# Third attention group in sixteen residues: VectorE's 32x32 transposes in place of TensorE's, values through DRAM

## The chip, the core and the metric

The kernel runs on one core of a Trainium2 chip. Its engines are named as in the profile: PE is TensorE (PEld its weight loads), DVE is VectorE, ACT is ScalarE, POOL is GpSimd, and SP is the engine whose queue issues nearly all DMAs. The metric is the device time of one execution in microseconds. Before the change the median of three runs is 1027.51 us (1027.5 to 1027.77).

## What is computed

One layer of a decoder trunk on 512 tokens of width 1024, all in float32: a normalization, one wide projection, three token mixers side by side (dilated attention, causal pooling, a state-space scan), gates, an output projection, a convolutional feed-forward layer and a last normalization. The change touches the attention alone. It has three groups of six heads of width 64; a group has a window and a dilation.

```python
ATTN_GROUPS = ((128, 1), (512, 4), (2048, 16))
...
    """Causal attention of each query t to keys t, t-d, ..., t-steps*d.
    Positions with the same residue mod d form a subsequence on which the pattern
    is a plain causal band of width `steps`; ..."""
...
    bias = bias_table[bucket].transpose(2, 0, 1).astype(jnp.float32)
    scale = 1.0 / math.sqrt(dh)
    scores = jnp.einsum("bhnqd,bhnkd->bhnqk", qb, kb).astype(jnp.float32) * scale + bias[:, None]
    scores = jnp.where(valid[None, None], scores, -jnp.inf)
    m = jnp.max(scores, axis=-1, keepdims=True)
    p = jnp.exp(scores - m)
    l = jnp.sum(p, axis=-1)
    o = jnp.einsum("bhnqk,bhnkd->bhnqd", p, vb.astype(jnp.float32)) / l[..., None]
    lse = m[..., 0] + jnp.log(l)
```

In the third group the dilation is 16, so each of 16 residues has 32 of the 512 tokens, and a query sees only keys of its own residue.

## The kernel before

**Projections and weights.** A product in float32 is made of three passes over parts of the operands: high by high, high by low and low by high (`mm3`, line 238, from which most rows of PE come). The weights go through a pipeline of jobs: SP fetches a block (`fetch`, line 184, tile `raw`), ACT writes its high part (`cast`, line 197, tile `wh`), DVE subtracts that from it (`lows`, line 217, tile `wl`), and PE multiplies. While job n runs, the weights of job n+1 are split, those of n+2 cast and those of n+3 fetched. Two buffers hold fetched blocks, so a fetch waits for the subtraction that frees one. SP issues its DMAs in order: what stands ahead of a fetch delays it.

**What runs beside them.** Smaller work is written as generators and advanced by `step()`, which is called after each chunk of a job (8 k-blocks of the three passes, 24 matmuls). A generator yields a phase, `ROWS`, `WHOLE` or `REST`, and these phases set the order of the matmuls of the generators of one step on PE. The order of instructions on PE, ACT, DVE and POOL is the order in which the program is written; that of SP is left to the planner.

**The third group (g = 2) before.** The tokens are put in four residues mod 4 of 128 tokens each: `perm`, `grouped` and `blocked` write and read queries, keys and outputs with a step of 4 elements. The scores of a head are four 128x128 blocks, one for each residue mod 4, and the bias holds a very negative number wherever query and key differ mod 16, which is in three of four places. For each head `item` in `attend` does this, in rising steps: the scores on PE (line 768, tile `ps`, for two heads at once), the bias added on DVE (line 783, tile `sb`), the negated maximum on DVE (line 787), the exponential with its sum on ACT (line 790); then, two steps later, the four 128x128 blocks are transposed on PE (line 797, tile `pt`) and copied back from PSUM (line 798, on DVE for even heads and on ACT for odd ones). After the second head of a pair PE multiplies with the values (line 811, tile `po`), and DVE copies the result out (line 816, tile `o`). The transposes and the outputs use the same four PSUM banks as the state-space scan that runs at the same time (`SM`; rows `py`, `pyo`, `pxs`, `pst`).

**Values and bias.** The values of groups two and three come out of PE with tokens as rows; `emit` in `v_pair` (line 646) moves each block of 128 rows by four DMAs from SBUF to SBUF, so that a tile `vr` holds one residue mod 4. The bias rows (`bias_rows`) are made on PE from a constant of 896 columns and the bias table (line 554), written to DRAM as `rdram` and spread by DMAs over the partitions (line 567), 128x2x128 for each pair of heads of group three.

Of the kernel before, what the change touches and what calls it, by code (L numbers as in the profile page):

```python
# [16 lines left out]
P = 128  # L17
# [20 lines left out]
C_GATE = C_DT + SH  # L38

R_OFF = (0, 384, 640)  # L40
R_LEN = (384, 256, 256)
R_ALL = 896
STEPS = (1, 1, 4)


def _bucket(dist):
# [7 lines left out]
def _constants():  # L54
    eye = np.eye(P, dtype=np.float32)
    tri = np.triu(np.ones((P, P), np.float32))
    hot = np.zeros((BUCKETS + 1, R_ALL), np.float32)
    for (window, dil), off, n, zero, step in zip(GROUPS, R_OFF, R_LEN, (255, 127, 127), STEPS):
        for j in range(n):
            rel = (zero - j) // step  # L60
            if (zero - j) % step == 0 and 0 <= rel <= window // dil:
                hot[_bucket(rel * dil), off + j] = 1.0
            else:
                hot[BUCKETS, off + j] = NEG
    ramp = np.ones((4, 16), np.float32)
    for g in range(4):
        w = 2 << g
        for t in range(w):
            ramp[g, t] = w / (t + 1.0)
    return {"c_eye": eye, "c_tri": tri, "c_hot": hot, "c_ramp": ramp}  # L70
# [13 lines left out]
def trunk(ctx: ExitStack, tc, out, x, rel_bias, ln1_g, w_in, b_gate, w_a, pool_w, pool_scale, w_b,  # L84
# [29 lines left out]
    def SM(name):  # L114
        return psum.tile([P, S], F32, name=name, tag="sm")
# [49 lines left out]
    def after(n, it):  # L165
        for _ in range(n):
            yield
        yield from it
# [176 lines left out]
    def sevens(quarter, c, side, W, emit):  # L345

        r1, r2, r3, r5 = {}, {}, {}, {}

        def job(j, load, form, use):
            def body(ws):
                wh, wl = ws
                parts = side(j)
                for i in range(2):
                    ps = MM("pb")
                    o = slice(i * P, (i + 1) * P)
                    mm3(ps[:, :c], lambda k: wh[:, k, :], lambda k: wl[:, k, :],
                        lambda k: parts[k][0][:, o], lambda k: parts[k][1][:, o], range(4), flip=True)
                    use(i, ps[:, :c])  # L360
                step()
            new = Job([load] if load is not None else [], 4, c, body)
            new.form = form
            if load is None:
                new.load = lambda: None
            return new

        def keep(r, name):
            def use(i, ps):
                r[i] = T(name)[:, :c]  # L370
                act.copy(r[i], ps)
            return use

        def p5(i, ps):
            keep(r5, "r5")(i, ps)
            dve.tensor_tensor(r2[i], r2[i], ps, OP.add)

        def p6(i, ps):
            dve.tensor_tensor(r1[i], r1[i], ps, OP.add)
            emit(0, 1, i, r1[i], r2[i])  # L380

        def p7(i, ps):
            r3[i] = T("r3")[:, :c]
# [12 lines left out]
        yield job(1, None, lambda: one.raw, p5)  # L396
        yield job(2, None, lambda: W[1], p6)
        yield job(3, None, lambda: W[0], p7)
        yield job("A22", None, lambda: diff(two.raw, two.raw, W[1]),
                  lambda i, ps: emit(1, 0, i, r3[i], ps))  # L400
# [128 lines left out]
    def bias_rows():  # L529


        relb, hot = T("relb"), [T(f"hot{i}") for i in range(2)]

        hr, two = [T(f"hotr{i}", F32R) for i in range(2)], T("relp", F32R)
        rh, rl = two[:, :18], two[:, 18:36]
        dve.memset(relb[:, :18], 1.0)
        sp.dma_start(relb[:BUCKETS, :18], rel_bias)
        sp.dma_start(hot[0][:BUCKETS + 1, :S], c_hot[:, :S])
        sp.dma_start(hot[1][:BUCKETS + 1, :R_ALL - S], c_hot[:, S:])

        def part(tiles, lo, n):
            i = lo // S
            return tiles[i][:, lo - i * S:lo - i * S + n]

        def rows():
            rv = [T(f"rv{i}") for i in range(2)]
            rd = dram.tile([HEADS, R_ALL], F32, name="rdram")
            ps_r = [SM("psr0"), SM("psr1")]
            for g, (off, n) in enumerate(zip(R_OFF, R_LEN)):
                lo = off  # L550
                while lo < off + n:
                    m = min(off + n, (lo // S + 1) * S) - lo
                    for r in (rh, rl):
                        pe.matmul(part(ps_r, lo, m)[:HEADS], r[:BUCKETS + 1, 6 * g:6 * g + 6],
                                  part(hr, lo, m)[:BUCKETS + 1], start=r is rh, stop=r is rl)
                    lo += m
            for i in range(2):
                m = (S, R_ALL - S)[i]
                dve.tensor_copy(rv[i][:HEADS, :m], ps_r[i][:HEADS, :m])
                sp.dma_start(rd[:, i * S:i * S + m], rv[i][:HEADS, :m])  # L560
            for i in range(6):
                b = T(f"b{i}")
                spans = ((0, 256, 0),) if i < 3 else ((1, P, 0), (2, P, 256))
                for g, width, at in spans:
                    src = bass.AP(tensor=rd.tensor, offset=rd.offset + R_OFF[g] + 2 * (i % 3) * R_ALL,
                                  ap=[[1, P], [R_ALL, 2], [1, width]])
                    sp.dma_start(b[:, at:at + 2 * width].rearrange("p (h c) -> p h c", h=2), src)
                bias.append(b)
            return
            yield  # L570

        def parts():
            n = BUCKETS + 1
            dve.tensor_copy(rh[:n], relb[:n, :18])
            dve.tensor_sub(rl[:n], relb[:n, :18], rh[:n].bitcast(F32))
            for i in range(2):
                m = (S, R_ALL - S)[i]
                dve.tensor_copy(hr[i][:n, :m], hot[i][:n, :m])

        return rows, parts  # L580

    def bias_of(g, h):
        if g == 0:
# [3 lines left out]


    def perm(ap, g):
        return ap if g == 0 else ap.rearrange("p (j r) -> p r j", r=4)  # L590

    def grouped(ap, g):

        return ap.rearrange("p (r j) -> p r j", r=4)[:, :, ::-1]

    def blocked(ap, g):
        return ap.rearrange("p (r j) -> p r j", r=4) if g == 0 else perm(ap, g)

    def plain(ap, g):
        return ap if g == 0 else ap.rearrange("p (r j) -> p r j", r=4)  # L600

    dtr = cpool.tile([P, 4, SH], F32, name="dtr")

# [23 lines left out]
    def v_pair():  # L627

        c, W = C_V + 384, []
        rows_ = lambda c0: w_in[:, c0:c0 + 384].rearrange("(k two p) c -> two p k c", two=2, p=P)  # L630
        quarter = lambda two, h: rows_(c + 384 * h)[two]

        def load():
            for two in range(2):
                W.append(ypool.tile([P, 4, S], F32, name="w3", tag="xs")[:, :, :384])
                sp.dma_start(W[two], quarter(two, 1))

        def emit(hi, right, i, a, ps):
            g, tb = 1 + right, 2 * hi + i
            t = T(f"v{g}")  # L640
            dve.tensor_tensor(t[:, :384], a, ps, OP.add)

            for n in range(4):
                if (g, n) not in V:
                    V[g, n] = T(f"vr{g}")
                sp.dma_start(V[g, n][32 * tb:32 * tb + 32, :384], t[n:P:4, :384])

        return load, sevens(quarter, 384, side_u, W, emit)

    def qk_jobs(g):  # L650
        for i in range(3):
# [92 lines left out]
    def attend(g):  # L744
# [7 lines left out]
        def item(h, nb, bank):  # L752
# [38 lines left out]
                               bias=nm[:, n, h:h + 1], accum_out=ls[:, n, h:h + 1])  # L791
            yield
            yield
            yield WHOLE
            pt = SM("pt")
            for o in range(0, total, P):
                pe.transpose(pt[:, o:o + P], sb[:, o:o + P], eye)  # L797
            (act.copy if h % 2 else dve.tensor_copy)(sb[:, :total], pt[:, :total])
            probs[h, nb] = sb


            if h % 2 == 0 or nb < len(banks) - 1 or g == 1 and c == 1:
# [665 lines left out]
    def program():  # L1468
# [7 lines left out]
        for i, job in enumerate(branch_jobs(1, w_b, YB, 8, more=range(7))):  # L1476
            if i == 3:
                yield Call(lambda: running.extend(after(p, sums_of_u(p)) for p in range(4)))
            yield job
        load, pair = v_pair()  # L1480
        yield Call(load)
        yield from gate_jobs(1, 0, SPLIT)
        loads, qk = qk_sevens(1)
# [3 lines left out]
                yield Call(loads)  # L1487
        yield from qk
        yield Call(lambda: attend(1))
        yield from gate_jobs(1, SPLIT)  # L1490
        yield from jobs_a(w_in, C_XBC, 12, uhk, ulk, KD, xbc_evac)
        yield Call(ssd_start)
# [72 lines left out]
        (b_gate[0].rearrange("(c p) -> c p", p=P), 24),  # L1565
        (pool_scale[0].rearrange("(c p) -> c p", p=P), 8)], "col")
    sp.dma_start(tri, c_tri)
    rows_of_bias, parts_of_bias = bias_rows()

    def row_squares(tb, ss, n=1, eng=dve):  # L1570

# [177 lines left out]
```

## Time and profile before

| | before |
|---|---|
| median of three runs | 1027.51 us (1027.5 to 1027.77) |
| span of the profiled execution | 1025.5 us |
| time around the span (median less span) | 2.0 us |
| PE busy | 1015.3 us, 99% of the span |
| DVE busy | 712.6 us, 69% |
| ACT busy | 489.9 us, 48% |
| mean granted clock of PE | 0.998 |

The profile is of one execution; its span runs from the first to the last instruction, and no other time of that execution is given, so it is set beside the median. A row of the timeline gives start, length, engine, line of the kernel, operation, the tile written and those read, and the shape; matmuls of one form that follow each other are merged, with their count. Because matmuls are pipelined, the length of a row on PE overlaps the next one: what a row costs is read from the start of the next. Idle time ahead of a row stands in brackets with what ended it. The third group's heads run between about 417 and 501 us of the span, among the gate and z projections and the state-space scan.

### The profile page before, as it was taken

Reading aid. Unit: us, or ns where it says so; the run is one execution under the profiler, and the core shown is the slowest. Engines: PE = TensorE matmul, PEld = TensorE weight load, DVE = VectorE, ACT = ScalarE, POOL = GpSimd, SP = SyncE. Lnnn points to the kernel's source line nnn. Section 1 sums busy time; section 2 is a strip of 40 time slices with the busy share of each in tenths; the row PEclk is TensorE's granted clock in tenths of the full one; section 3 lists DMA queues with packets and bytes.
Section 4 is the critical chain, followed back from the end, with each engine's and each line's share of the span. In section 5 each row is a group of like instructions: output and inputs, shape, how many; then the busy total and the mean of one; then the engine's idle time right before and its main releaser. Section 6 shows DMA issues by size and latency. Waiting matters only on the chain.

```text
span 1025.5 us, 13278 instructions
## 1 busy us (share of the span) xinstructions
PE 1015.3 (99%) x5282; PEld 859.1 (84%) x5282; DVE 712.6 (69%) x948; ACT 489.9 (48%) x786; POOL 128.9 (13%) x108
## 2 busy tenths in 40 slices
PE   8999999999999999999999999999999999999997
PEld 8998878899888888888888888898888888888885
DVE  6563566788756659776789666768778768685756
ACT  5432545454674364557566234644444434433434
POOL 1770000000000001000043501102111100111002
PEclk9999999999999999999999999999999999999999
DMA  8444312034422354552254526543232233321322
GB/s 261 146 126 142 107 59 76 31 98 129 124 83 82 98 146 106 144 143 67 60 157 161 164 83 220 182 141 98 84 121 82 87 119 116 130 82 42 123 82 82
DMA packets 113356, 117.62 MB, mean 115 GB/s; under 512 B 5235, under 2 KB 97206, under 8 KB 113295
## 3 DMA queue, kind: packets, MB, share of 16 engines
q1 hardware_dynamic: 112703, 115.92, 36.5%
q8 instruction: 41, 0.67, 0.3%
q10 hardware_dynamic: 592, 0.86, 0.2%
q14 instruction: 20, 0.16, 0.1%
HBM read 112.97 MB, written 2.22 MB: 112 GB/s over the span
## 4 chain that ended last, share of the span: by engine, by line
PE 98%; DMA 1%; DVE 0%; ACT 0%; ACTq 0%; issue 0%
PE pa L238 36%; PE pu L238 22%; PE pb L238 12%; PE pd L238 7%; PE pqk L238 6%; PE pq L238 3%; PE pa L1596 2%; PE ps L768 1%; PE pu L1398 1%; PE pt L797 1%; PE ppw L238 1%; PE po L811 1%; PE py L1096 1%; DMA xin<-in_x_dram 1%; PE pyo L1103 1%; PE pst L1084 0%
## 5 line engine op out<-in xcount | busy, mean ns | idle before, releaser
L217 DVE TENSOR_TENSOR wl<-raw,wh 128x2048 fp32r<-128x2048 f32 (+3 forms) x95 | 220.0, 2316 | 49.0 <-ACT wh L197 40.9
L197 ACT CAST wh<-raw 128x1024 fp32r<-128x1024 f32 (+4 forms) x187 | 186.5, 1017 | 43.3 <-DVE raw L342 18.0
L1293 DVE SCALAR_TENSOR_TENSOR hc<-pu,fcol,hc 128x510 f32<-128x510 f32 x88 | 65.9, 748 | 56.4 <-ACT hc L1290 54.8
L238 PE MATMUL pa<-uh,wh 128*128 128x512 f32 x384 | 97.5, 396 | 0.0
L238 PE MATMUL pa<-ul,wh 128*128 128x512 f32 x384 | 94.9, 389 | 0.0
L238 PE MATMUL pa<-uh,wl 128*128 128x512 f32 x384 | 94.8, 389 | 0.0
L238 PEld LDWEIGHTS pa<-ul,wh 128*128 128x128 f32 x384 | 72.1, 188 | 15.2
L238 PEld LDWEIGHTS pa<-uh,wl 128*128 128x128 f32 x384 | 72.1, 188 | 15.0
L238 PE MATMUL pu<-uh,wh 128*128 128x512 f32 (+1 forms) x352 | 83.6, 379 | 0.0
L238 PE MATMUL pu<-uh,wl 128*128 128x512 f32 (+1 forms) x352 | 83.5, 379 | 0.0
L238 PE MATMUL pu<-ul,wh 128*128 128x512 f32 (+1 forms) x352 | 83.5, 379 | 0.0
L238 PEld LDWEIGHTS pa<-uh,wh 128*128 128x128 f32 x384 | 70.3, 188 | 13.9
L238 PEld LDWEIGHTS pu<-uh,wl 128*128 128x128 f32 x352 | 64.2, 188 | 12.5
L238 PEld LDWEIGHTS pu<-ul,wh 128*128 128x128 f32 x352 | 64.2, 188 | 12.5
L238 PEld LDWEIGHTS pu<-uh,wh 128*128 128x128 f32 x352 | 64.1, 188 | 12.4
L1290 ACT ACTIVATE hc<-pu,fcol,fcol 128x512 f32<-128x512 f32 x40 | 31.2, 779 | 79.0 <-PE pu L238 79.0
L1298 POOL TENSOR_TENSOR hc<-hc 128x512 f32<-128x512 f32 x22 | 30.8, 1401 | 289.0 <-DVE hc L1293 252.0
L1079 POOL TENSOR_TENSOR st<-st,dts 128x512 f32<-128x512 f32 x4 | 7.2, 1804 | 378.8 <-ACT st L1087 318.2
L790 ACT ACTIVATE sb<-sb,nmls 128x128 f32<-128x128 f32 (+1 forms) x72 | 30.0, 418 | 28.2 <-DVE nmls L787 16.2
L1190 ACT ACTIVATE sg<-pa,col 128x512 f32<-128x512 f32 x24 | 16.5, 688 | 39.9 <-PE pa L238 35.8
L1295 ACT ACTIVATE hc<-hc 128x512 f32<-128x512 f32 x22 | 13.9, 633 | 39.9 <-DVE hc L1293 39.9
L933 DVE SCALAR_TENSOR_TENSOR xs<-pa,col,xs 128x509 f32<-128x509 f32 (+2 forms) x24 | 18.0, 749 | 18.0 <-ACT xs L929 17.4
(389 smaller groups left out, 1869.5 us busy)
## 6 DMA issues: line engine op xcount, KB each, us to landing
raw<-in_w_in_dram SPq DMA_DIRECT2D x25, 1024.0 KB, 5.9
raw<-in_ffn_w_up_dram SPq DMA_DIRECT2D x22, 1024.0 KB, 5.1
raw<-in_w_o_dram SPq DMA_DIRECT2D x8, 1024.0 KB, 6.5
raw<-in_ffn_w_down_dram SPq DMA_DIRECT2D x8, 1024.0 KB
raw<-in_w_in_dram SPq DMA_DIRECT2D x14, 512.0 KB, 3.9
raw<-in_w_in_dram SPq DMA_DIRECT2D x6, 768.0 KB
raw<-in_w_b_dram SPq DMA_DIRECT2D x4, 1024.0 KB, 5.0
al<-ad SPq DMA_DIRECT2D x16, 256.0 KB, 7.1
```

Of the source, the lines that this page charges most:

```text
L197: (other.tensor_copy if other and i else act.copy)(job.high[:, :, o], job.raw[:, :, o])
L217: (eng or dve).tensor_tensor(l[:, :, o], job.raw[:, :, o], h[:, :, o].bitcast(F32), OP.subtract)
L238: pe.matmul(ps, l, r, start=first and n == 0, stop=last and n == total - 1, skip_group_check=onto)
L768: pe.matmul(pss[i][:, o:o + w * P], q[r, n * P:(n + 1) * P], k[r, kb * P:(kb + w) * P], start=True, stop=True)
L790: act.activation(sb[:, off:off + w * P], sb[:, off:off + w * P], AF.Exp, bias=nm[:, n, h:h + 1], accum_out=ls[:, n, h:h + 1])
L933: dve.scalar_tensor_tensor(t[:, sh:], ps[:, :S - sh], col[:, o_cw + 12 * k + m:o_cw + 12 * k + m + 1], t[:, sh:], OP.mult, OP.add)
L1190: act.activation(s, ps, AF.Sigmoid, bias=col[:, o:o + 1])
L1290: act.activation(t, ps, AF.Identity, bias=ff["c1"][:, ff["b"] + m:ff["b"] + m + 1], scale=fw(2, m))
L1293: dve.scalar_tensor_tensor(t[:, sh:], ps[:, :S - sh], fw(k, m), t[:, sh:], OP.mult, OP.add)
L1295: act.activation(t, t, AF.Silu)
L1298: pool.tensor_tensor(a, a, t, OP.mult)
L1596: pe.matmul(first[2 * n + j][:, lo:hi], a[:, k, j * P:(j + 1) * P], b[:, k, lo:hi], start=a is wh and b is uh and k == 0, stop=a is wl and ...
```

## The change

The tokens of the third group are put in sixteen residues of 32 consecutive entries: within a block of 128 (one residue mod 4) stand four sub-blocks of 32, one for each residue mod 16. A score block of 128x128 then holds its live entries in four 32x32 blocks on the diagonal, and the bias is very negative elsewhere, so the exponential there is zero. Such a block is transposed whole when each of its 32x32 blocks is transposed in its place, which is what VectorE's transpose does. So in group three `item` no longer transposes on PE and copies back, but writes a new tile `sbt` with one DVE transpose of 128x512, in the phase `REST` of the same step.

The values of group three are written to DRAM (`vdram`, one DMA for each block of 128 rows) and read back later, every sixteenth row, by four DMAs of 32 rows for each tile `vr`. The bias tile of group three is filled by a memset on DVE and four DMAs of 32x2x32 on its diagonal; the constant is cut from 896 to 704 columns. Both come from generators `residues`, which start two steps after the second group's heads are queued. The scores and the product with the values keep their shapes, 128x128.

```diff
-R_LEN = (384, 256, 256)
-R_ALL = 896
-STEPS = (1, 1, 4)
+R_LEN = (384, 256, 64)
+R_ALL = 704
...
-                spans = ((0, 256, 0),) if i < 3 else ((1, P, 0), (2, P, 256))
-                for g, width, at in spans:
-                    src = bass.AP(tensor=rd.tensor, offset=rd.offset + R_OFF[g] + 2 * (i % 3) * R_ALL,
-                                  ap=[[1, P], [R_ALL, 2], [1, width]])
-                    sp.dma_start(b[:, at:at + 2 * width].rearrange("p (h c) -> p h c", h=2), src)
+                g, width = (0, 256) if i < 3 else (1, P)
+                sp.dma_start(b[:, :2 * width].rearrange("p (h c) -> p h c", h=2),
+                             spans(rd, g, i % 3, P, width))
                 bias.append(b)
+            bias.append(rd)
...
+        def residues():
+            rd = bias.pop()
+            for c in range(3):
+                b = bias[3 + c][:, 256:]
+                dve.memset(b, NEG)
+                for a in range(0, P, 32):
+                    sp.dma_start(b[a:a + 32].rearrange("p (h c) -> p h c", h=2)[:, :, a:a + 32],
+                                 spans(rd, 2, c, 32, 32))
+                yield
...
     def perm(ap, g):
-        return ap if g == 0 else ap.rearrange("p (j r) -> p r j", r=4)
+        if g == 0:
+            return ap
+        if g == 1:
+            return ap.rearrange("p (j r) -> p r j", r=4)
+        return ap.rearrange("p (j a r) -> p r a j", a=4, r=4)
+
+    def plain(ap, g):
+        if g == 0:
+            return ap
+        if g == 1:
+            return ap.rearrange("p (r j) -> p r j", r=4)
+        return ap.rearrange("p (r a j) -> p r a j", r=4, a=4)
 
     def grouped(ap, g):
 
-        return ap.rearrange("p (r j) -> p r j", r=4)[:, :, ::-1]
+        return plain(ap, g)[:, :, :, ::-1] if g == 2 else plain(ap, 1)[:, :, ::-1]
...
+        vd = dram.tile([S, 384], F32, name="vdram")
...
             dve.tensor_tensor(t[:, :384], a, ps, OP.add)
+            if g == 2:
+                sp.dma_start(vd[tb * P:(tb + 1) * P, :], t[:, :384])
+                return
...
+        def residues():
+            for n in range(4):
+                t = V[2, n] = T("vr2")
+                for a in range(4):
+                    sp.dma_start(t[32 * a:32 * a + 32, :384], vd[4 * a + n:S:16, :])
+                yield
...
-            yield WHOLE
-            pt = SM("pt")
-            for o in range(0, total, P):
-                pe.transpose(pt[:, o:o + P], sb[:, o:o + P], eye)
-            (act.copy if h % 2 else dve.tensor_copy)(sb[:, :total], pt[:, :total])
-            probs[h, nb] = sb
+            if g == 2:
+                yield REST
+                probs[h, nb] = T("sbt")
+                dve.transpose(probs[h, nb], sb)
+            else:
+                yield WHOLE
+                pt = SM("pt")
+                for o in range(0, total, P):
+                    pe.transpose(pt[:, o:o + P], sb[:, o:o + P], eye)
+                (act.copy if h % 2 else dve.tensor_copy)(sb[:, :total], pt[:, :total])
+                probs[h, nb] = sb
...
         yield Call(lambda: attend(1))
+        yield Call(lambda: running.extend(after(2, f()) for f in (residues_of_v, residues_of_bias)))
```

More of the change, by code (lines that the diff above doesn't have):

```diff
@@ L57, in _constants @@
     hot = np.zeros((BUCKETS + 1, R_ALL), np.float32)
-    for (window, dil), off, n, zero, step in zip(GROUPS, R_OFF, R_LEN, (255, 127, 127), STEPS):
+    for (window, dil), off, n, zero in zip(GROUPS, R_OFF, R_LEN, (255, 127, 31)):
         for j in range(n):
-            rel = (zero - j) // step
-            if (zero - j) % step == 0 and 0 <= rel <= window // dil:
+            rel = zero - j
+            if 0 <= rel <= window // dil:
                 hot[_bucket(rel * dil), off + j] = 1.0
@@ L562, in rows, with spans @@
                 b = T(f"b{i}")
-                spans = ((0, 256, 0),) if i < 3 else ((1, P, 0), (2, P, 256))
-                for g, width, at in spans:
-                    src = bass.AP(tensor=rd.tensor, offset=rd.offset + R_OFF[g] + 2 * (i % 3) * R_ALL,
-                                  ap=[[1, P], [R_ALL, 2], [1, width]])
-                    sp.dma_start(b[:, at:at + 2 * width].rearrange("p (h c) -> p h c", h=2), src)
+                g, width = (0, 256) if i < 3 else (1, P)
+                sp.dma_start(b[:, :2 * width].rearrange("p (h c) -> p h c", h=2),
+                             spans(rd, g, i % 3, P, width))
                 bias.append(b)
+            bias.append(rd)
             return
             yield
+        def spans(rd, g, c, high, width):
+            return bass.AP(tensor=rd.tensor, offset=rd.offset + R_OFF[g] + 2 * c * R_ALL,
+                           ap=[[1, high], [R_ALL, 2], [1, width]])
+        def residues():
[7 more added lines that the diff above has]
+                yield
         def parts():
@@ L578, in parts @@
                 dve.tensor_copy(hr[i][:n, :m], hot[i][:n, :m])
-        return rows, parts
+        return rows, parts, residues
     def bias_of(g, h):
@@ L589, in perm @@
     def perm(ap, g):
-        return ap if g == 0 else ap.rearrange("p (j r) -> p r j", r=4)
+        if g == 0:
[9 more added lines that the diff above has]
+        return ap.rearrange("p (r a j) -> p r a j", r=4, a=4)
     def grouped(ap, g):
-        return ap.rearrange("p (r j) -> p r j", r=4)[:, :, ::-1]
+        return plain(ap, g)[:, :, :, ::-1] if g == 2 else plain(ap, 1)[:, :, ::-1]
     def blocked(ap, g):
-        return ap.rearrange("p (r j) -> p r j", r=4) if g == 0 else perm(ap, g)
-    def plain(ap, g):
-        return ap if g == 0 else ap.rearrange("p (r j) -> p r j", r=4)
+        return plain(ap, 1) if g == 0 else perm(ap, g)
     dtr = cpool.tile([P, 4, SH], F32, name="dtr")
@@ L646, in emit @@
                 sp.dma_start(V[g, n][32 * tb:32 * tb + 32, :384], t[n:P:4, :384])
-        return load, sevens(quarter, 384, side_u, W, emit)
+        def residues():
[4 more added lines that the diff above has]
+                yield
+        return load, sevens(quarter, 384, side_u, W, emit), residues
     def qk_jobs(g):
@@ L1479, in program @@
             yield job
-        load, pair = v_pair()
+        load, pair, residues_of_v = v_pair()
         yield Call(load)
@@ L1567, in trunk @@
     sp.dma_start(tri, c_tri)
-    rows_of_bias, parts_of_bias = bias_rows()
+    rows_of_bias, parts_of_bias, residues_of_bias = bias_rows()
     def row_squares(tb, ss, n=1, eng=dve):
```

## The prediction, made before the changed kernel ran

> **What bounds the kernel now.** I read the page first (busy time, chain), then the waits of PE, then the chain and the timeline around the third attention group, and last what DVE, SP and ACT have to spare there.
>
> ```profile
> span 1025.5 us, 13278 instructions
> PE 1015.3 (99%) x5282; PEld 859.1 (84%) x5282; DVE 712.6 (69%) x948; ACT 489.9 (48%) x786; POOL 128.9 (13%) x108
> PE 98%; DMA 1%; DVE 0%; ACT 0%; ACTq 0%; issue 0%
> ...
> PE uT L1613 <- DVE diag L1625: 2.1, 2, 1.6
> PE pa L1555 <- DVE ones L1546: 1.1, 1, 1.1
> ```
>
> The third line is the chain that ended last: 98% of it is PE. The two rows behind it are all that the waits of PE list, 3.2 us, and both lines (L1555, L1613) belong to the start of the kernel. From there PE runs from one matmul to the next. So a matmul taken out shortens the time by the distance between its neighbours' starts, and work added on DVE, ACT or SP costs nothing until it makes PE wait. The median of the runs is 1027.51 us and the profiled span 1025.5: 2.0 us lie around the span, which I leave as they are, so what the span loses comes off 1027.51.
>
> **Removed from PE: six groups of four transposes.** In the changed program's order the six groups `pt` of the third attention group (line 797) are gone and nothing takes their place on PE; all other rows of PE keep their order and, but for one pair below, their shapes. What a group costs is not its busy time, since matmuls overlap, but the difference between a stretch of starts with it and one without it. There are three kinds of place.
>
> ```profile
> 476.49 1.98 PE L238 MATMUL pa<-uh,wl 128*128 128x512 f32 x8
> 478.30 0.60 PE L797 MATMUL pt<-eye,sb 128*128 128x128 f32 x4
> 478.66 2.08 PE L238 MATMUL pa<-uh,wh 128*128 128x512 f32 x8
> 480.58 1.98 PE L238 MATMUL pa<-ul,wh 128*128 128x512 f32 x8
> 482.39 0.84 PE L238 MATMUL pa<-uh,wl 128*128 128x512 f32 x3
> ...
> 446.72 1.16 PE L768 MATMUL ps<-k,q 64*128 64x128 f32 x16
> 447.82 0.65 PE L797 MATMUL pt<-eye,sb 128*128 128x128 f32 x4
> ...
> 450.16 1.98 PE L238 MATMUL pa<-ul,wh 128*128 128x512 f32 x8
> ...
> 269.70 1.16 PE L768 MATMUL ps<-k,q 64*128 64x128 f32 x16
> ...
> 272.75 1.98 PE L238 MATMUL pa<-ul,wh 128*128 128x512 f32 x8
> ...
> 486.20 1.16 PE L1103 MATMUL pyo<-xcv,st 128*128 128x128 f32 x8
> 487.19 0.60 PE L797 MATMUL pt<-eye,sb 128*128 128x128 f32 x4
> ...
> 489.47 0.84 PE L238 MATMUL pa<-ul,wh 128*128 128x512 f32 x3
> ...
> 471.83 1.16 PE L1103 MATMUL pyo<-xcv,st 128*128 128x128 f32 x8
> ...
> 474.67 1.52 PE L238 MATMUL pa<-ul,wh 128*128 128x512 f32 x6
> ```
>
> Columns: start, length, engine, line, operation, tiles. Kind one, between long products: from the `pa` at 476.49 to the one at 480.58 are 4.09 us with `pt`; eight undisturbed products take 482.39 - 480.58 = 1.81, so without `pt` it would be 3.62: 0.47 us. That holds more than the four transposes themselves (478.66 - 478.30 = 0.36): the product behind them is 0.11 slower to get going. Four of the six groups are of this kind (two follow `pst`, a product of the same shape): 4 x 0.47 = 1.88. Kind two, behind the scores: 450.16 - 446.72 = 3.44 with, 272.75 - 269.70 = 3.05 without: 0.39, since the scores too leave a slow start behind. Kind three, behind `pyo`: 489.47 - 486.20 = 3.27 with, 474.67 - 471.83 = 2.84 without: 0.43. The sum is 1.88 + 0.39 + 0.43 = 2.70 us. If the slow start stayed behind in all six places, 6 x 0.36 = 2.2 would be left: the lower end.
>
> **The bias rows.** The constant is cut from 896 to 704 columns, so the last pair of the eight small matmuls has 64 columns in place of 256.
>
> ```profile
> 63.14 0.92 PE psr L554 x8
> ```
>
> The eight stream 2 x 896 columns in 0.92 us; 2 x 192 of 1792 are 0.20 us at most, nothing at least, if their length is fixed. I take 0.1. In all 2.8 us.
>
> **DVE: six 32x32 transposes, three memsets; three copies fewer.** ACT loses its three copies of `sb<-pt`. No row shows a 32x32 transpose.
>
> ```profile
> L798 DVE COPY sb<-pt x12: 553/683/692, 132.0 to 490.4; 128x512 f32<-128x512 f32 x9, 128x384 f32<-128x384 f32 x3
> L816 DVE COPY o<-po x3: 1080/1094/1110, 455.9 to 500.3; 128x512 f32<-128x512 f32 x3
> L663 DVE COPY k<-pqk x6: 681/688/692, 88.4 to 404.2; 128x512 f32<-128x512 f32 x6
> L1546 DVE MEMSET ones<- x1: 165/165/165, 0.8 to 0.8; 128x128 f32 x1
> ...
> 447.92 0.69 DVE L783 SCALAR_TENSOR_TENSOR sb<-ps,b 128x512 f32<-128x512 f32 x1 [0.56 <-PE ps L768]
> ...
> 455.89 1.08 DVE L816 COPY o<-po 128x512 f32<-128x512 f32 x1 [4.37 <-PE po L811]
> 491.56 0.68 DVE L1139 TENSOR_TENSOR xs<-xs,zs 128x512 f32<-128x512 f32 x1
> 494.87 2.29 DVE L217 TENSOR_TENSOR wl<-raw,wh 128x2048 fp32r<-128x2048 f32 x1 [2.63 <-ACT wh L197]
> ```
>
> The nearest row is the copy of the same 128x512 elements, 0.68 us, which I take; the far end is 2.3 us, the length of the 128x2048 subtraction. Six at 0.68 less three copies are 2.0 us more on DVE. The two places where a transpose is new and its reader nearest have cover: the second head's is queued just ahead of the row at 447.92, before which DVE stood 0.56 us, and 4.37 us of idle time follow before `o<-po`; the last head's comes behind the row at 491.56, and 2.63 idle us follow. At 0.68 neither delays the product that reads it. At 2.3 the two transposes around the row at 491.56 would add 1.6 + 2.3 = 3.9 us to DVE, 1.3 more than its 2.63 idle us, and the subtraction behind them would be as much later: that is where the cover ends. The wait is new on DVE (for the exponential of ACT), but PE's transposes waited for the same one; behind it on DVE stand the next head's scores and the next weights' subtraction `wl`. Three memsets of 128x256 are at most 2 x 0.165 each, 1 us in all, beside the second group's scores; none is on PE's path.
>
> **Address patterns.** Queries, keys and output of the third group now step over 16 elements where they stepped over 4. Reading PSUM in steps costs nothing so far: `k` shows 681 to 692 ns in six runs, three plain and three in steps of 4. Writing SBUF in steps does: `o<-po` takes 1.09 where the plain copy takes 0.68. I take 1.09, the nearest row, for steps of 16 too; the far end is another such doubling, 1.9 us. That matters in one place only:
>
> ```profile
> 454.97 0.90 PE po L811 x16
> ...
> 455.89 1.09 DVE o L816
> 456.98 0.04 issue
> 457.03 0.66 PE pxs L1051 x4
> ```
>
> Here the chain leaves PE: `pxs` wants the PSUM bank that `o<-po` empties, and starts as soon as it ends. In the changed program `pxs` waits for the same copy. Every 0.1 us more on it is 0.1 us more of the time; at 1.9 us it is 0.8.
>
> The Trainium skill, page "SBUF — State Buffer", section "Specifications (TRN2)", says that SBUF has 16-byte lines and that each step onto a new line pays. The rows agree with it (1.09 against 0.68 at a step of 16 bytes), and by it 64 bytes would cost no more than 16, so its sum is mine.
>
> **SP and the DMAs.** For the values four writes of 128x384 and sixteen reads of 32x384 take the place of sixteen moves; for the bias twelve of 32x2x32 the place of three of 128x2x128. In the changed order the reads and the bias pieces stand behind the weight fetch that SP now issues at 282.31, and nineteen of them stand ahead of the next one, now at 294.55.
>
> ```profile
> 234.74 10.82 SPq L646 DMA_DIRECT2D vr<-v  x16
> 282.31 0.37 SPq L184 DMA_DIRECT2D raw<-in_w_in_dram  x1
> 294.55 0.37 SPq L184 DMA_DIRECT2D raw<-in_w_in_dram  x1
> 309.96 0.37 SPq L184 DMA_DIRECT2D raw<-in_w_in_dram  x1
> 309.99 1.04 ACT L197 CAST wh<-raw 128x1024 fp32r<-128x1024 f32 x1
> ...
> raw<-in_w_in_dram SPq DMA_DIRECT2D x25, 1024.0 KB, 5.9
> vr<-v SPq DMA_DIRECT2D x32, 48.0 KB, 4.5
> ```
>
> A small move holds SP 10.82 / 16 = 0.68 us, so nineteen take 12.9, from 282.7 to 295.6: the fetch goes out 1 us late. It lands 5.9 later, at 301.5, and the cast that reads it runs at 309.99: 8.5 us of cover left. The nine others, 6.1 us, stand ahead of the fetch at 309.96, 14 us after that. I take 0.
>
> **Forecast.** 1027.51 - 2.70 - 0.1 = 1024.7 us. About 0.2%, or 2.05 us, is what a measurement of this kernel can tell from no change: the limit is 1025.45.
>
> **Rivals.**
> 1. The output copy in steps of 16 holds `pxs` longer (1.9 us in place of 1.09): 1024.7 + 0.8 = 1025.5, within 0.2%. For it: the price is known for one step only, and the chain already runs through it. Against: it would need a second doubling. With the low end of the transposes (0.5 less saved) it is 1026.0. Chance 0.11, with all else that eats 0.75 us or more without eating everything.
> 2. SP falls behind. The moves from DRAM may go out slower than those from SBUF, since SP also waits for earlier ones to land: landing took 4.5 us, and the bias pieces are 128 bytes each. The cover of the fetch ends where it goes out at 309.99 - 5.9 = 304.1, that is at (304.1 - 282.7) / 19 = 1.13 us per move. At 1.5 us it goes out at 311.2, 7.1 us late, and ACT's cast, DVE's subtraction and PE behind them with it: 1024.7 + 7.1 = 1031.8, slower. Against it: 0.68 us for moves of the same size. Chance 0.07. The Trainium skill, page "DMA: Bandwidth & Descriptors", section "Specifications", gives 512 bytes as the least for full rate, with a read-modify-write below it, which speaks for this rival; no run here shows a piece of 128 bytes yet.
> 3. The change does less on PE than it says: excluded, since the groups are gone from the program's order.
>
> **Numbers.** Forecast 0.82, rival one 0.11, rival two 0.07. The range: below, `pxs` starts 1.16 us after `po` ends, while `pyo`, which lies between, needs 0.99 from start to start (486.20 to 487.19), so some 0.2 us of standing may go, and the other 0.1 of the bias rows: 1024.4; less the spread of the runs (1027.5 to 1027.77) once for each kernel, 0.5: 1023.9. Above, rival one with some spread: 1025.9. What lies above is rival two.
>
> **What would show it.** Right: PE busy and span both down by 2.5 to 3 us, no new row among PE's waits, the transpose on DVE at 0.6 to 1.1 us, `o<-po` near 1.1, the idle time before the cast on ACT unchanged. Wrong: a wait of `po` for `sbt` or for `vr`, `pxs` starting late behind a longer copy, or a cast waiting for its `raw` near 310 us.

## The result, and the profile after

The changed kernel takes 1024.34 us (median of 7 runs, 1023.96 to 1024.70), the kernel before beside it 1027.27 us (median of 7, 1026.93 to 1027.77): a ratio of 0.997, 95% interval 0.9959 to 0.9981. That is 2.9 us less, where 2.8 were forecast: a small change, about 0.3%, but outside that interval. The profiled execution took 1024.48 us and has a span of 1022.7 us: 1.8 us lie around the span, and the span itself lost 2.8.

The page of the changed kernel:

```profile
span 1022.7 us, 13259 instructions
PE 1012.5 (99%) x5258; PEld 857.0 (84%) x5258; DVE 713.1 (70%) x954; ACT 488.5 (48%) x783; POOL 130.2 (13%) x108
PE 98%; DMA 1%; DVE 0%; ACT 0%; ACTq 0%; issue 0%
```

PE issues 24 instructions fewer (six groups of four) and is busy 2.8 us less; DVE, which took the work over, is busy 0.5 us more. (The prediction's 2.0 us for the transposes show in the stretch between the two `pst` rows below, where DVE is busy 48.11 us in place of 46.26; outside it other rows of DVE were shorter in sum.) PE still carries 98% of the chain. The waits of PE (us in all, times, longest):

```profile
PE uT L1650 <- DVE diag L1662: 2.3, 2, 1.5
PE pa L1592 <- DVE ones L1583: 1.1, 1, 1.1
```

These are the same two as before, at the start of the kernel: no new wait of PE for the turned probabilities or for the values' rows. The timeline of PE around the third group, cut to the rows that stand against those of the prediction; then the first and the last `pst` row of the kernel before:

```profile
432.17 0.39 PE L1120 MATMUL pst<-xdh,bth 128*128 128x512 f32 x1
...
446.41 1.16 PE L799 MATMUL ps<-k,q 64*128 64x128 f32 x16
...
449.46 1.98 PE L237 MATMUL pa<-ul,wh 128*128 128x512 f32 x8
...
475.25 1.98 PE L237 MATMUL pa<-uh,wl 128*128 128x512 f32 x8
...
478.88 1.98 PE L237 MATMUL pa<-ul,wh 128*128 128x512 f32 x8
...
484.49 1.16 PE L1139 MATMUL pyo<-xcv,st 128*128 128x128 f32 x8
...
487.34 1.98 PE L237 MATMUL pa<-ul,wh 128*128 128x512 f32 x8
...
497.52 0.61 PE L859 MATMUL pst<-eye,nmls 128*38 128x128 f32 x4
```

```profile
431.99 0.39 PE L1084 MATMUL pst<-xdh,bth 128*128 128x512 f32 x1
...
500.15 0.62 PE L823 MATMUL pst<-eye,nmls 128*38 128x128 f32 x4
```

Between long products: 478.88 - 475.25 = 3.63 (4.09 before), behind the scores 449.46 - 446.41 = 3.05 (3.44), behind `pyo` 487.34 - 484.49 = 2.85 (3.27). 3.63 is twice the 1.81 of undisturbed products: the slow start went with the transposes. From the first `pst` row to the last are 65.35 us; before, the same two rows are 68.16 apart. The whole saving of 2.81 lies in this stretch; what is earlier and later in the kernel cancels (in this execution PE was 0.35 us later than in the one before when it reached the bias rows, these took nearly half of that back, so that 0.18 was left at the first `pst` row, and the part behind the last is 0.17 shorter).

The groups of DVE that are new or changed (ns: least, median, most), and the chain of waits at the two other places that the prediction priced (start, length):

```profile
L828 DVE STREAM_TRANSPOSE sbt<-sb x6: 704/706/712, 434.5 to 490.4; 128x512 f32<-128x512 f32 x6
L852 DVE COPY o<-po x3: 1036/1048/1049, 455.2 to 497.7; 128x512 f32<-128x512 f32 x3
```

```profile
63.49 0.74 PE psr L553 x8
...
455.19 1.05 DVE o L852
...
456.28 0.66 PE pxs L1087 x4
```

A transpose of 128x512 in blocks of 32x32 takes 0.706 us, about what a copy of that size takes. The copy in steps of 16 takes 1.05 where steps of 4 took 1.09, and `pxs` still starts as it ends. And the small DMAs, in the timeline of SP, with the two rows of DVE and ACT on which the fetch at 295.17 hangs:

```profile
282.97 2.00 SPq L676 DMA_DIRECT2D vr<-vdram  x4
...
291.71 1.73 SPq L580 DMA_DIRECT2D b<-rdram  x4
293.48 0.89 SPq L676 DMA_DIRECT2D vr<-vdram  x2
295.17 0.39 SPq L183 DMA_DIRECT2D raw<-in_w_in_dram  x1
```

```profile
292.86 2.28 DVE L216 TENSOR_TENSOR wl<-raw,wh 128x2048 fp32r<-128x2048 f32 x1
```

```profile
310.17 1.03 ACT L196 CAST wh<-raw 128x1024 fp32r<-128x1024 f32 x1
```

The nineteen moves are through at 294.4. The fetch goes out as the subtraction `wl` ends (292.86 + 2.28 = 295.14; before, 292.24 + 2.28 = 294.52), since that frees the buffer it writes; the cast stands where it stood.

### The profile page after: what moved, and what is told of

Its sections match the earlier page's. It is cut to its first block, busy times and chain, and to the rows that moved or that the text cites. A ratio compares the mean times of both kernels' runs of the same rounds, so it can differ in the third digit from the quotient of the medians.

```text
span 1022.7 us, 13259 instructions
## 1 busy us (share of the span) xinstructions
PE 1012.5 (99%) x5258; PEld 857.0 (84%) x5258; DVE 713.1 (70%) x954; ACT 488.5 (48%) x783; POOL 130.2 (13%) x108
## 4 chain that ended last, share of the span: by engine, by line
PE 98%; DMA 1%; DVE 0%; ACT 0%; ACTq 0%; issue 0%
PE pa L237 36%; PE pu L237 22%; PE pb L237 12%; PE pd L237 7%; PE pqk L237 6%; PE pq L237 3%; PE pa L1633 2%; PE ps L799 1%; PE pu L1434 1%; PE ppw L237 1%; PE po L847 1%; PE pt L833 1%; PE py L1132 1%; DMA xin<-in_x_dram 1%; PE pyo L1139 1%; PE pst L1120 0%
```

## The experiments

The forecast came out, so the runs test its reasons: that the six groups alone are the gain, that DVE and SP hide what was put on them, and where that cover ends (cover is the idle time between the end of some work and the first moment at which PE would wait for it; PE stands when it is idle in such a wait). "Theory A" is the prediction's own reading or what the trace after made of it, as each text says. All times stand against 1024.3 us of the changed kernel; the kernel before, run again beside each set, had medians of 1027.32 to 1027.50 us. Comments behind # in the cuts of code are this text's.

### Only the transposes undone, all or half

```
-            if g == 2:
+            if g == 3:              # all six heads on PE again
+            if g == 2 and h % 2:    # the even heads on PE again
                 ...
                 dve.transpose(probs[h, nb], sb)
```

> The changed kernel, but the probabilities of the third group are again turned by PE and copied back; the residues of 32 tokens, the steps of 16, the rows through DRAM and the shorter bias rows stay. Theory A (the time came from PE's six groups of transposes, 2.70 us): 1024.3 + 2.7 = 1027.0 us, six rows of pt on PE in the third group, with start-to-start stretches of 4.09, 3.44 and 3.27 us around them again. Rival B (the time came from the rest: the order of queues, the DMAs, the bias rows): 1024.3 to 1024.6 us.

> The changed kernel, but the even heads of the third group (0, 2, 4) are turned by PE, the odd ones by VectorE. Theory A (each group pays its own place, nothing else): two places of kind one, at 0.47 us, and the one behind pyo, at 0.43: 1024.3 + 1.37 = 1025.7 us. Rival B (the gain is a step, not a sum: a wait that goes only when the last transpose is gone, or with the first): 1027.0 or 1024.3 us.

All on PE: 1027.15 us (11 runs, 1026.59 to 1027.55; ratio to the kernel before 0.9997, 0.9988 to 1.0006). Half: 1025.52 us (11 runs; 0.9981, 0.9973 to 0.9990). The timeline of PE with half of them, around heads three (DVE) and four (PE):

```profile
475.91 1.98 PE L237 MATMUL pa<-uh,wl 128*128 128x512 f32 x8
...
479.54 1.98 PE L237 MATMUL pa<-ul,wh 128*128 128x512 f32 x8
...
485.15 1.16 PE L1139 MATMUL pyo<-xcv,st 128*128 128x128 f32 x8
486.15 0.60 PE L833 MATMUL pt<-eye,sb 128*128 128x128 f32 x4
...
488.43 1.99 PE L237 MATMUL pa<-ul,wh 128*128 128x512 f32 x8
```

479.54 - 475.91 = 3.63 without a group, 488.43 - 485.15 = 3.28 with one: each head pays its own place. 2.8 us back for six (2.7 expected) and 1.2 for three (1.37 expected) is a sum, not a step. Theory A holds. The residues, the way through DRAM, the steps of 16 and the shorter bias rows together bring nothing that these runs can tell: with PE transposing the kernel stands level with the one before, within about 1 us.

### More work on DVE: each transpose three, five and seven times

```
-                dve.transpose(probs[h, nb], sb)
+                for _ in range(3):      # and 5, and 7
+                    dve.transpose(probs[h, nb], sb)
```

> The changed kernel with each of the six VectorE transposes done three times over: 2 x 0.706 = 1.41 us more on DVE per head, 8.5 us in all. Theory A (DVE's work there is covered: up to about 2.3 us per transpose by the idle times in the trace): 1024.3 us, within 0.2, no new row among PE's waits. Rival B (the transposes delay the products, the scores or the bank that pxs wants): up to 8.5 us more, 1032.8 us; if only the output copy ahead of pxs is pushed, 1.4 us more, 1025.7 us.

> The changed kernel with each of the six VectorE transposes done five times over: 4 x 0.745 = 2.98 us more on DVE per head. Theory A (the cover ends a little above three, as the idle times on DVE say): o ahead of pxs is late by about 0.6 + 2.98 - 2.18 = 1.4 us, and the last transpose ends near 497.1 where po wants it at 496.5: 0.6 to 1.2 us; in all 2.0 to 2.6 us, 1026.3 to 1026.9 us, unless the standing makes the granted clock drop, which adds 1 to 2 us each time. Rival B (no end of the cover before seven): 1024.3 us. Rival C (each us of DVE beyond three counts in all six heads): 1024.3 + 6 x 1.49 = 1033.3 us.

> The changed kernel with each of the six VectorE transposes done seven times over: 6 x 0.706 = 4.24 us more on DVE per head, 25.4 us in all. Theory A (each delay runs along DVE's queue until idle time eats it): the second head's pushes o ahead of pxs by 4.24 plus 1.85 left from the first, less 2.18 of idle time: 3.9 us; the last two heads push the product po by 8.5 less the idle time there: about 4.9 us; 1024.3 + 8.8 = 1033.1 us, with new waits of PE for o and for sbt or wl of 3 to 5 us each. Rival B (all of it on the path): 1049.7 us. Rival C (nothing there is near the path): 1024.3 us.

Three times: 1024.44 us (6 runs, 1023.99 to 1024.76), no new row among PE's waits. Five times: 1026.95 us (11 runs, 1025.74 to 1029.41). Seven times: 1038.89 us (4 runs, 1037.99 to 1039.37). Two rows of DVE with three (its timeline: start, length, what ended the idle time ahead), then the waits of PE with five, then with seven:

```profile
448.07 2.20 DVE L829 STREAM_TRANSPOSE sbt<-sb 128x512 f32<-128x512 f32 x3
...
455.35 1.04 DVE L853 COPY o<-po 128x512 f32<-128x512 f32 x1 [1.58 <-PE po L848]
```

```profile
PE pxs L1088 <- DVE o L853: 0.9, 1, 0.9
...
PE po L848 <- DVE sbt L829: 0.6, 1, 0.6
```

```profile
PE po L848 <- DVE sbt L829: 8.6, 2, 5.2
...
PE pxs L1088 <- DVE o L853: 1.4, 1, 1.4
```

2.20 us per head are free, and 1.58 us of idle time are still left ahead of the copy that sets `pxs`; 3.69 us (five) cost 2.6 us in the median. The profiled execution is the fastest of those eleven (1025.74 us, 1.4 us more), and its two new waits, 0.9 and 0.6 us, are the two ways that theory A named; what the slower ones lost beyond that, up to 1029.41 us, no trace shows. So the cover ends between 2.20 and 3.69 us, and the real 0.706 us is far inside it. At seven theory A was right in kind and wrong in size (8.8 expected, 14.5 found). It had overlooked the wait of the first `po` for its own transpose (3.4 us), ahead of the `pxs` wait that it did name; together PE stood 10.0 us. The rest is the clock, in the windows of that run (columns: stretch, length, busy time of PE, PEld, DVE, ACT and POOL, granted clock, DMA):

```profile
458.00:462.00 4.00, 2.77 (x22) 2.31 (x20) 3.96 (x5) 2.92 (x9) 1.14 (x1) 0.60 0.01 2
462.00:466.00 4.00, 3.85 (x12) 3.23 (x13) 3.93 (x10) 1.63 (x3) 0.07 (x1) 0.54 0.94 296
```

After PE had stood it was granted half of its clock for 6.8 us, the whole of it again from 465.7 on. The 4.5 us that the waits leave open (14.5 - 10.0) are put down to this and to the same fall around the second place, where the clock was at 0.50 from 506.6 to 513.4.

### The output copy: three and five times, and without its steps

```
-                (dve.tensor_copy if g == 2 else act.copy)(blocked(o, g), grouped(po, g))
+                for _ in range(3 if g == 2 else 1):      # and 5
+                    (dve.tensor_copy if g == 2 else act.copy)(blocked(o, g), grouped(po, g))
```

The third kernel copies plainly and lets POOL step later:

```
+                if g == 2:
+                    dve.tensor_copy(o, po)
...
+                if g == 2:
+                    pool.tensor_tensor(blocked(wb, g), grouped(OT[g, c], g), blocked(wb, g), OP.mult)
+                    OT[g, c] = wb
```

> The changed kernel with each of the three output copies of the third group done three times over: 2 x 1.05 = 2.10 us more per copy. Theory A (rival one's mechanism: only the first of the three sets the start of pxs, and there every us of it is a us of the time): 1024.3 + 2.1 = 1026.4 us, and a wait of about 2.3 us of pxs for o. Rival B (all three are on the path): 1024.3 + 6.3 = 1030.6 us. Rival C (pxs finds another bank in time): 1024.3 us.

> The changed kernel with each of the three output copies of the third group done five times over: 4 x 1.04 = 4.2 us more per copy. Theory A (a us on the first copy is a us of the time, and PE stands for about 4.4 us before pxs): 1024.3 + 4.2 = 1028.5 us if the granted clock stays at 1.00 behind the standing, as it did behind 2.86 us; Rival B (the clock falls to about 0.5 for some 3 to 4 us behind it, as behind 1.94, 3.41 and 5.22 us in other runs): 1.2 to 2 us more, 1029.7 to 1030.5 us.

> The changed kernel with the third group's output copied out of PSUM in PSUM's own order, without steps, and put in order later by the multiplication on POOL, which takes its steps there. Theory A (steps in the SBUF output are what makes the copy 1.05 us instead of 0.68, and its end sets pxs until pyo does): copies of 0.65 to 0.70 us, pxs without its 0.24 us of waiting, 1024.1 us: 0.2 us, less than the runs can tell. Rival B (the length comes from reading PSUM, not from the steps): copies of 1.05 us still, no change. Rival C (steps on POOL cost more there and the later products wait for it): slower, with a wait behind POOL.

Three times: 1027.33 us (11 runs, 1026.27 to 1028.76), 3.0 more. Five times: 1032.19 us (5 runs, 1031.95 to 1034.79), 7.9 more. Plain: 1024.17 us (5 runs, 1023.52 to 1026.31; ratio to the kernel before 0.9966, 0.9953 to 0.9980). The PE timeline of the first, two rows of its DVE timeline, and its window behind the standing (granted clock 1.00); then the waits of PE and a window of the second (granted clock 0.71):

```profile
455.09 1.16 PE L1140 MATMUL pyo<-xcv,st 128*128 128x128 f32 x8
459.11 0.63 PE L1088 MATMUL pxs<-eye,xs 128*128 128x128 f32 x4 [2.86 <-DVE o L853]
```

```profile
449.98 0.88 DVE L1103 TENSOR_SCALAR al<-al,acs 128x128 f32<-128x128 f32 x4 [1.83 <-DMA al<-ad]
...
455.84 3.12 DVE L853 COPY o<-po 128x512 f32<-128x512 f32 x3
```

```profile
459.00:463.00 4.00, 3.89 (x19) 3.32 (x20) 3.93 (x9) 0.00 (x0) 0.00 (x0) 1.00 0.92 266
```

```profile
PE pxs L1088 <- DVE o L853: 4.3, 1, 4.3
PE pss L1196 <- DVE sql L1190: 2.1, 1, 2.1
```

```profile
461.00:465.00 4.00, 4.00 (x15) 3.21 (x14) 3.93 (x13) 0.00 (x0) 0.00 (x0) 0.71 0.13 33
```

Of the three copies only the first is on the path, as theory A says. With three copies in a row, `pxs` starts 4.02 us after `pyo`, 2.81 later than the 1.21 of the changed kernel: 2.1 are the two copies, the rest is that DVE reached them 0.65 us later (455.84, not 455.19), behind a decay transfer `al<-ad` that landed late: its reader starts at 449.98, in the changed kernel at 447.06, and from there DVE has no idle time up to the copy. The clock stayed whole in this execution. The eleven runs fall in two groups: seven took 1026.27 to 1027.44 us at a mean granted clock of 0.998 or 0.999, as the profiled one did, four took 1028.05 to 1028.76 at 0.996. Theory A's 1026.4 is met by the first group alone. With five, 4.3 us of standing, about 1.5 us of slower clock behind it and 2.1 us of a second wait (`pss`, 60 us later, for DVE work that the two other copies had pushed) make the 7.9; rival B had the clock, neither had `pss`.

The plain copy in the group view, and its `pxs` in the PE timeline:

```profile
L853 DVE COPY o<-po x3: 691/691/692, 454.5 to 496.7; 128x512 f32<-128x512 f32 x3
```

```profile
454.36 1.16 PE L1146 MATMUL pyo<-xcv,st 128*128 128x128 f32 x8
455.36 0.60 PE L1094 MATMUL pxs<-eye,xs 128*128 128x128 f32 x4
```

0.69 in place of 1.05: the order costs the difference, and reading PSUM as such does not. The plain copy drops two things, the steps of 16 in which `blocked` writes SBUF and the backward order in which `grouped` reads PSUM. That the steps are the dear one is likely, since `k<-pqk`, three of whose six copies read PSUM in steps of 16, takes 0.68 to 0.69 in all six, but reading backward was not tried alone. On POOL the multiplication takes 2.0 us in steps, and nothing on PE waits for it, so rival C is out. `pxs` follows `pyo` by 1.00 us in place of 1.21, so 0.2 us is gained on the path in this trace. The times cannot tell that kernel from the changed one; it is the lowest median of the study, and clearly below the kernel before.

### More small moves on SP

```
                 for a in range(4):
                     sp.dma_start(t[32 * a:32 * a + 32, :384], vd[4 * a + n:S:16, :])
+                if n == 0:
+                    for i in range(48):     # 10 elements each; and 40, of 12
+                        a, o = i % 4, 384 + 10 * (i // 4)
+                        sp.dma_start(t[32 * a:32 * a + 32, o:o + 10], vd[4 * a:S:16, :10])
```

> The changed kernel with 48 further small moves (32 x 10 elements each, from the values in DRAM into unused columns) queued on SP behind the first four of the residues, ahead of the weight fetch at 295.17. At 0.43 us each they hold SP 20.6 us; with those already there the fetch goes out near 311 and lands near 317. Theory A (the prediction's rival two: the cast at 310.17 is late by as much, and PE with it): 7 us late, 1031 us. Rival B (PE reads that cast only at 323.39, and ACT has nothing to do between 311.2 and 315.3, so the cover is larger than the prediction had it): 1024.3 to 1026 us, with the cast on ACT late by 5 to 8 us all the same.

> The changed kernel with 40 further small moves (32 x 12 elements) ahead of the weight fetch at 295.17. At the 0.508 us per extra move that the run with 48 showed, the fetch goes out near 310.9, and the cast that reads it, at 310.17 so far, runs near 316.8: 6.6 us late. Theory A (the prediction's rival two: PE is late by as much as the cast): 1031 us. Rival B (PE has about 8.8 us of cover behind the cast, as with 48 moves, where the cast was 10.7 late and PE waited 1.94): 1024.3 us, no wait of po for sb, no slower clock.

48 moves: 1027.99 us (11 runs, 1026.29 to 1028.99), 3.7 more. 40 moves: 1024.31 us (6 runs, 1023.96 to 1025.00), nothing. SP and ACT with 40, then SP, ACT, PE and a window (granted clock 0.50) with 48:

```profile
311.86 0.39 SPq L183 DMA_DIRECT2D raw<-in_w_in_dram  x1
```

```profile
317.66 1.05 ACT L196 CAST wh<-raw 128x1024 fp32r<-128x1024 f32 x1 [7.25 <-DMA raw<-in_w_in_dram]
```

```profile
284.91 24.38 SPq L680 DMA_DIRECT2D vr<-vdram  x48
...
315.00 0.39 SPq L183 DMA_DIRECT2D raw<-in_w_in_dram  x1
```

```profile
320.90 1.05 ACT L196 CAST wh<-raw 128x1024 fp32r<-128x1024 f32 x1 [10.90 <-DMA raw<-in_w_in_dram]
```

```profile
324.10 1.30 PE L851 MATMUL po<-sb,vr 128*64 128x128 f32 x14 [1.94 <-ACT sb L838]
```

```profile
325.00:328.00 3.00, 3.00 (x11) 2.11 (x10) 2.96 (x3) 0.00 (x0) 0.00 (x0) 0.50 0.97 328
```

The cast may be 7.5 us late (317.66, not 310.17) and PE does not notice. When it is 10.7 us late, PE does not wait for the weights but for `sb`, a copy that stands behind the cast on ACT: 1.94 us, and the slower clock behind it makes up the rest of the 3.7. Of the eleven runs four took 1026.29 to 1026.74 us, about the wait alone; the other seven, the profiled one among them, took 1027.59 to 1028.99. Theory A, that PE is late by as much as the cast, fell in both runs; rival B was right with 40, and with 48 right about the cover but short by 2 us.

### The values' rows without the way through DRAM

```
-                sp.dma_start(vd[tb * P:(tb + 1) * P, :], t[:, :384])
+                for n in range(4):
...
+                    for a in range(4):
+                        lo = 32 * a + 8 * tb
+                        sp.dma_start(V[g, n][lo:lo + 8, :384], t[4 * a + n:P:16, :384])
...
-                for a in range(4):
-                    sp.dma_start(t[32 * a:32 * a + 32, :384], vd[4 * a + n:S:16, :])
```

> The changed kernel without the way through DRAM: the values' rows go from SBUF to SBUF as in the kernel before, but in the finer residues that takes 64 moves of 8 x 384 elements where there were 16 of 32 x 384. Theory A (SP is held about 0.65 us by each, whatever its size, and they stand ahead of the weight fetches at 231 and 246.59): the first fetch goes out about 15 us late, the later one about 28 us, against covers of some 2 and 7 us: 15 to 25 us slower, 1040 to 1050 us. Rival B (SP has room there, the way through DRAM brings nothing): 1024.3 us.

1059.6 us (4 runs, 1058.82 to 1059.85; ratio to the kernel before 1.0306, 1.0292 to 1.0321). SP's timeline and PE's waits:

```profile
228.05 40.06 SPq L669 DMA_DIRECT2D vr<-v  x64
268.21 0.39 SPq L183 DMA_DIRECT2D raw<-in_w_in_dram  x1
```

```profile
PE pq L237 <- ACT wh L196: 31.4, 1, 31.4
```

Right in kind, short in size: 0.63 us each as expected, but all 64 moves stand ahead of the first fetch, not half of them, so it is 37 us late and PE stands 31.4 us, then 0.4 us more for a subtraction `wl`. The rest of the 35.3 us is put down to the clock, which was granted at 0.50 until 280.8. Of the two ways tried, only four large writes to DRAM and sixteen reads back give residues of 32 without a loss.

## Why the prediction was right, point by point

- **The bound.** PE's row-to-row distance was the time, before and after. Right: no wait of PE is new.
- **The six groups, 2.70 us.** Measured by the same differences: 0.48 three times (the two behind `pst` and the last), 0.46, 0.39 and 0.42, 2.71 in all. Right, and undoing them alone gave it back. The lower end (the slow start stays) did not occur.
- **The bias rows, 0.1 us.** Under-sized: 0.92 became 0.74, so 0.18, near its upper bound of 0.20.
- **The transposes.** 0.706 for 0.68. The prediction let the cover end at about 2.3 us per transpose; the runs say between 2.20 (free) and 3.69 (not). It named the wrong reader: not the subtraction `wl`, but `pxs` behind `o<-po`, and `po` itself came late first.
- **The output copy, 1.09 us.** 1.05. Rival one needed a second doubling with the wider step, and the step made no difference; its mechanism, a us of copy for a us of time, is shown by the copy done three times. The Trainium skill, page "SBUF — State Buffer", section "Specifications (TRN2)", says that each crossing to a new 16-byte line is paid for. The copies agree with it, 0.69 plain against 1.09 at steps of 16 bytes and 1.05 at 64; that a wider step costs no more is what these rows show, not the page's words. The 0.2 us of standing before `pxs` that the range allowed for went only by 0.05.
- **SP.** "A small move holds SP 0.68 us" was too much: 0.43 to 0.50 for the moves from DRAM where SP did not stand (1.73 / 4, 2.00 / 4). Within the first four bias pieces (3.31 us) SP did stand, 1.7 us until a weight block had landed, so rival two's step that SP waits for earlier transfers occurred; it fitted into the room there was. The fetch went out 0.6 us late (1 us expected), and not for SP's sake: in both kernels it goes out as `wl` ends.
- **Rival two.** It did not happen, and its price was wrong. Its step "ACT's cast, DVE's subtraction and PE behind them with it" fails: a fetch at 311.9 costs nothing, one at 315.0 makes PE wait 1.94 us, so the cover ends near 315.0 - 1.94 = 313, not at 304.1: (313 - 282.7) / 19 = 1.6 us per move, not 1.13. At its 1.5 us per move this fetch would have gone out inside the cover; what the nine moves behind it would do at that price was not tried. That pieces of 128 bytes would be dear was not seen at SP (1.73 us for four of them, 2.00 for four of 1536 bytes).
- **The sum.** 2.71 + 0.18 + 0.05 is 2.94; the medians differ by 2.93, with an interval of about 1 us to each side, and the profiled spans by 2.8. That the first two meet to 0.01 us is luck: the start of the kernel alone differs by 0.35 us between the two traces. The time itself came out 0.36 us below the forecast of 1024.7, mostly because the kernel before, run again beside the changed one, was 0.24 us faster than the 1027.51 that the forecast starts from.

## What to carry to other kernels

Where one engine's instructions follow each other without a gap, price a removed instruction as the difference of start-to-start stretches with and without it, not by its length: that gave 2.70 for 2.71, with up to 0.11 us of a slow start per place that no row names. Follow a late buffer to the instruction that first makes the bounding engine wait, in the order of each queue between: the cast that was 7.5 us late cost nothing, and what finally cost was another instruction queued behind it. And a small copy that empties a PSUM bank can be on the path where a far larger load is not: here its order was worth 0.36 us of its length, and 0.2 us of that on the path.

## What was not expected of the hardware

Standing costs PE more than its length, but not always. Behind 1.94 us (48 moves) and 4.33 us (five copies) of standing the granted clock fell to 0.50 for 3.4 us, around 3.41 us with 1.37 of a second wait after it and around 5.22 us (both with seven transposes) for 6.8 us, and about 1.5 to 3 us more were lost each time; behind 2.86 us (three copies) it stayed at 1.00.

The traces also show when the clock can change. With seven transposes, read in windows of 0.04 us, it falls at 458.82, rises at 465.65, falls at 506.61 and rises at 513.44. These are 6.83, 40.96 and 6.83 us apart, which is 2, 12 and 2 steps of 3.413 us. Its changes with 48 moves, with five copies and without the way through DRAM lie whole steps apart as well, the fall at the very end of each kernel included (205 steps after the first fall with 48 moves, 166 with five copies). So in each of these executions the clock changed only on a grid of 3.413 us, and where a wait lies on the grid can matter: the 1.94 us lay within one step (321.4 to 324.8), while the grid of the run with three copies, counted back from the fall at its end, cuts the 2.86 us at 457.2 into 0.95 and 1.91. 1.91 and 1.94 are so close that the standing within a step need not be all that counts; what else does was not tried. The two groups among the runs of one kernel, with three copies and with 48 moves, fit a grid that lies differently in each execution, but only one execution of each was traced.

The Trainium skill, page "TensorE: Matmul & The Clock Gate", section "HAM oscillation — how this bites in real kernels", warns of idle gaps over about 3.4 us; here 1.94 us was enough once, and the measurement decides. Its account of a window that runs free of the kernel (section "Part 1: The HAM clock gate (the "warmup" mystery)") agrees with the grid of these traces.

The queue's price of a small DMA was higher for moves out of SBUF than for moves out of DRAM: 0.63 us each for 64 moves of 8x384 and 0.68 for the moves of 32x384 before, both from SBUF, against 0.51 for 48 of 32x10 and 0.43 to 0.50 for those of the changed kernel, from DRAM. What sets it was not tried: source, shape and place in the kernel changed together.
